# The mean square of the attention heads' outputs: two fp32r passes for each pair of blocks instead of fp32 products for a whole head

## The chip, the cores and the metric

The kernel runs on one core of one Trainium2 chip. The core has a matrix engine (TensorE, in the profile PE, with its weight loads as PEld), VectorE (DVE), ScalarE (ACT), GpSimd (POOL) and a queue of DMA issues (SyncE, SP). Each engine works through its own list of instructions in order, and waits on semaphores for the others. The metric is the time of one execution on the device in microseconds; lower is better.

## The reference, cut to what matters

One layer of a streaming encoder: an RMSNorm, a projection into eleven parts, a gated linear attention (GLA) branch, a differential attention branch, and their merge. The prompt has 1024 frames, the sample 32. The change touches one spot of the differential branch, the RMSNorm over the 128 channels of each head's output:

```python
def rmsnorm(x, g):
    xf = x.astype(F32)
    y = xf * lax.rsqrt(jnp.mean(xf * xf, axis=-1, keepdims=True) + EPS) * g.astype(F32)
    return y.astype(x.dtype)
...
    attn = p[:, :, 0] - lam * p[:, :, 1]
    return jnp.einsum('bhqk,bkhe->bqhe', attn, v.astype(F32))
...
    yd = (rmsnorm(o_diff.astype(x.dtype), diff_subln_g) * (1.0 - lambda_init)).reshape(B, T, DIFF_VAL) * jax.nn.silu(dg)
```

For each head (8) and each of the 1024 prompt frames, the mean of 128 squares is needed, then its inverse root, which scales the head's output before `w_proj_diff`.

## The kernel before, in words

Most products are done as three fp32r passes: each fp32 operand is split in a high part (rounded to fp32r, made on ACT) and a low part (the rest, a subtraction on DVE or POOL), and high x high, low x high and high x low are added up in PSUM. Channels lie on the 128 partitions, frames on the free axis.

The stages are: normalisation and the value projections (to about 200 us), GLA with the projections that it needs (to about 600), differential attention (to about 1190), then the two output projections and the last product. In GLA and differential attention, several threads share TensorE: the attention itself (`diff_main`), the sample's attention (`sample_thread`) and a filler of projections (`fill`, three passes of 352 columns for each of 8 blocks of channels, lines 465 to 467, 24 passes to a PSUM bank, two such banks). A small planner, `Order`, writes the order of TensorE: a step of a thread says what it costs, which events it needs and with which lag (the table `W`), and which PSUM banks it takes; the planner keeps a clock of these numbers and picks the first thread that is ready. TensorE is then run in that order as written. The other engines are ordered by the compiler's scheduler from priorities and the order in which the program was written.

One head of the differential attention, for 8 blocks of 128 frames: scores of both softmaxes (lines 883 and 884), the row maxima and the exponentials (887 on DVE, 889 on ACT), the difference of the two (892 to 894 on DVE), transposes (931) with the split of the transposed part (933 on ACT, 934 on DVE), and after each second block the value product of the pair (944 to 946) into a bank of the kind "o", of which there is one. ACT reads this bank twice: the squares go to `sqo` (947), the values to `osb` (948). At the end of a head, `diff_fin` averages the squares over the partitions: a product with a matrix whose entries are all 1/128 (`one_h`), twice 512 columns in fp32 (859), each into the one "o" bank; ACT reads one row of the result (860), and SP stores the 1024 averages (862). Then DVE multiplies the whole `osb` by the gate (865, 128x1024), and SP stores it. In `diff_main` the steps of `diff_fin` come after the next head's first scores. The values of the next head are split just then, the high part on ACT (912), the low part on POOL (913).

The sample thread, once for two heads, transposes its probabilities in two groups (1006), which ACT and DVE (1008, 1009) add up, before its value products (1018).

After the attention, the averages of all heads are read back, turned into scales on ACT, spread over the partitions (`rsb`) and multiplied into the outputs (1141) ahead of the second output projection (443 to 445). The first output projection (`pg_first`, 1099 to 1101) reads the GLA branch's gated tiles, split by 1069 (ACT) and 1070 (DVE).

## Time and profile before

| | us |
|---|---|
| median of 3 runs | 1483.13 |
| lowest, highest | 1480.83, 1486.48 |
| the profiled execution | 1483.59 |
| its span | 1481.9 |

The granted clock of TensorE over the profiled execution is 0.99 of full speed. In the lists, a row of the order of time gives the start, the duration, the engine, the line and the operation, what is written and read, and in brackets the idle time of the engine in front of it with what ended it. A row of a group gives the count, the busy time, the mean duration in ns, and the idle time in front. A row of stretches gives the length of the stretch, the busy time (and instructions) of PE, PEld, DVE, ACT and POOL, the granted clock, the DMA share and GB/s. The starts and ends of matmuls overlap by their pipeline, so the time that a row of passes takes is read from the distance of their starts.

### The profile page before, as it was taken

How to read it: one execution, taken by the hardware profiler on the slowest of the kernel's cores; microseconds unless marked ns; L12 is line 12 of the kernel's file. 1: busy time of each engine (PE TensorE's matmuls, PEld its weight loads, DVE VectorE, ACT ScalarE, POOL GpSimd, SP SyncE). 2: the span in 40 equal slices, each digit the busy share in tenths (PEclk: the TensorE clock that was granted, in tenths of full speed). 3: DMA queues.
4: the chain of work that ended last, by engine and by line, in shares of the span. 5: the costliest groups of instructions: out<-in, count | busy, mean ns of one | idle time of the engine just before them, and what ended most of it. 6: DMA issues, size and time to landing. Idle time of an engine off the chain costs nothing.

```text
span 1481.9 us, 22365 instructions
## 1 busy us (share of the span) xinstructions
PE 1422.6 (96%) x8848; PEld 1327.6 (90%) x8848; DVE 786.6 (53%) x1464; ACT 601.0 (41%) x1262; POOL 298.4 (20%) x186
## 2 busy tenths in 40 slices
PE   8999999989999999899999999999899899999997
PEld 6787789889989899899989998998899799999997
DVE  5702005755565343576767767678665535455415
ACT  5612114535344232455555555555455432221311
POOL 1200002222213224123222222222221111122001
PEclk9999999999999999999999999999999999999999
DMA  8621111122222233323232333223322278633205
GB/s 310 205 105 38 45 45 48 56 74 68 81 70 73 70 120 108 90 62 106 72 108 60 106 86 96 69 83 90 92 68 81 97 264 302 223 131 129 103 1 192
DMA packets 66742, 156.58 MB, mean 106 GB/s; under 512 B 10008, under 2 KB 28568, under 8 KB 65600
## 3 DMA queue, kind: packets, MB, share of 16 engines
q1 hardware_dynamic: 66624, 155.01, 32.3%
q8 instruction: 74, 1.21, 0.3%
q14 instruction: 44, 0.36, 0.1%
HBM read 104.39 MB, written 40.04 MB: 97 GB/s over the span
## 4 chain that ended last, share of the span: by engine, by line
PE 51%; DVE 6%; DMA 4%; ACT 2%; issue 1%; POOL 1%; SPq 0%; DVEq 0%; POOLq 0%; ACTq 0%
PE ps_w L465 9%; PE ps_w L466 9%; PE ps_w L467 9%; PE ps_w L444 2%; PE ps_w L443 2%; PE ps_w L445 2%; PE ps_s L884 2%; PE ps_t L931 2%; PE ps_s L883 2%; DMA ydr<-ydd 2%; PE ps_c L1193 2%; PE ps_c L1195 2%; PE ps_c L1194 2%; PE po L945 1%; PE po L946 1%
## 5 line engine op out<-in xcount | busy, mean ns | idle before, releaser
L465 PE MATMUL ps_w<-X,wh 128*128 128x352 f32 x1344 | 453.8, 338 | 8.5 <-DVE sg L478 3.2
L466 PE MATMUL ps_w<-X,wl 128*128 128x352 f32 x1344 | 438.2, 326 | 0.0
L467 PE MATMUL ps_w<-X,wh 128*128 128x352 f32 x1344 | 436.4, 325 | 0.0
L435 POOL TENSOR_TENSOR wl<-wr,wh 128x1024 fp32r<-128x1024 f32 x72 | 179.5, 2493 | 661.8 <-ACT wh L433 528.6
L465 PEld LDWEIGHTS ps_w<-X,wh 128*128 128x128 f32 x1344 | 255.8, 190 | 13.6 <-issue 4.9
L466 PEld LDWEIGHTS ps_w<-X,wl 128*128 128x128 f32 x1344 | 256.1, 191 | 1.2 <-issue 1.2
L467 PEld LDWEIGHTS ps_w<-X,wh 128*128 128x128 f32 x1344 | 255.1, 190 | 0.0
L889 ACT ACTIVATE p<-ps_s,nm 128x256 f32<-128x256 f32 (+7 forms) x128 | 94.6, 741 | 59.1 <-DVE ps_s L885 31.1
L286 PE MATMUL ps_v<-wh,X 128*128 128x512 f32 x248 | 97.6, 393 | 0.6 <-DVE X L225 0.6
L287 PE MATMUL ps_v<-wl,X 128*128 128x512 f32 x248 | 98.0, 395 | 0.0
L433 ACT ACTIVATE wh<-wr 128x1024 fp32r<-128x1024 f32 x72 | 75.9, 1054 | 54.6 <-PE ps_w L467 30.4
L285 PE MATMUL ps_v<-wh,X 128*128 128x512 f32 x248 | 97.9, 395 | 0.0
L887 DVE TENSOR_REDUCE nm<-ps_s 128x1 f32<-128x256 f32 (+7 forms) x128 | 94.8, 747 | 2.7
L272 DVE TENSOR_TENSOR vo<-ps_v,vo 32x512 f32<-32x512 f32 x4 | 2.7, 679 | 139.9 <-ACT vo L271 139.9
L885 DVE MEMSET ps_s<- 64x64 f32 x128 | 14.3, 112 | 115.8 <-PE ps_s L884 114.2
L650 POOL TENSOR_TENSOR vl<-vr,vh 128x512 fp32r<-128x512 f32 (+1 forms) x20 | 24.8, 1242 | 222.8 <-DVE t L516 160.3
L883 PE MATMUL ps_s<-k,q 128*128 128x512 f32 (+2 forms) x192 | 68.0, 362 | 1.2 <-DMA k<-k 1.2
L884 PE MATMUL ps_s<-kl,q 128*128 128x512 f32 (+2 forms) x192 | 63.8, 348 | 3.9 <-DMA kl<-kl 3.4
L268 ACT ACTIVATE vo<-ps_v 128x512 f32<-128x512 f32 x32 | 19.1, 596 | 114.2 <-PE ps_v L287 113.8
L933 ACT ACTIVATE ah<-ps_t 128x512 fp32r<-128x512 f32 (+2 forms) x96 | 46.9, 488 | 43.6 <-PE ps_t L931 43.0
L934 DVE TENSOR_TENSOR al<-ps_t,ah 128x512 fp32r<-128x512 f32 (+2 forms) x96 | 53.1, 554 | 18.6 <-ACT ah L933 17.3
L444 PE MATMUL ps_w<-Y,wl 128*128 128x352 f32 x192 | 62.2, 324 | 0.0
(319 smaller groups left out, 2960.9 us busy)
## 6 DMA issues: line engine op xcount, KB each, us to landing
wr<-w SPq DMA_DIRECT2D x72, 512.0 KB
thd<-gate SPq DMA_DIRECT2D x16, 528.0 KB
xn<-xn SPq DMA_DIRECT2D x16, 512.0 KB
wr<-wv SPq DMA_DIRECT2D x16, 512.0 KB
newk<-rr SPq DMA_DIRECT2D x8, 528.0 KB
ygr<-ygd SPq DMA_DIRECT2D x8, 528.0 KB
tha<-thd SPq DMA_DIRECT2D x8, 528.0 KB
ydr<-ydd SPq DMA_DIRECT2D x8, 528.0 KB
```

Of the source, the lines that this page charges most:

```text
L285: mm(ps, xk[:, 0, t0 : t0 + P], wh[:, k, :], start=(k == 0), stop=False)
L286: mm(ps, xk[:, 1, t0 : t0 + P], wh[:, k, :], start=False, stop=False)
L287: mm(ps, xk[:, 0, t0 : t0 + P], wl[:, k, :], start=False, stop=(k == KT - 1))
L435: nc.gpsimd.tensor_tensor(wl, wr, wh.bitcast(F32), op=ALU.subtract)
L444: mm(ps[:, :n], wl[:, k, :], src[k][:, 0, t0 : t0 + n], start=False, stop=False)
L465: mm(ps[:, :n], wh[:, k, :], src[k][:, 0, t0 : t0 + n], start=(k == 0), stop=False)
L466: mm(ps[:, :n], wl[:, k, :], src[k][:, 0, t0 : t0 + n], start=False, stop=False)
L467: mm(ps[:, :n], wh[:, k, :], src[k][:, 1, t0 : t0 + n], start=False, stop=(k == KT - 1))
L883: mm(ps[:, n0 : n0 + n], qs[m][:, qsl], ks[m][:, n0 : n0 + n], start=True, stop=False)
L884: mm(ps[:, n0 : n0 + n], qs[m][:, qsl], kls[m][:, n0 : n0 + n], start=False, stop=True)
L887: ve.tensor_reduce(nm, ps[:, 0:w], axis=AX.X, op=ALU.max, negate=True)
L889: act(p[:, 0:w], ps[:, 0:w], AF.Exp, bias=nm, accum_out=sm[:, m : m + 1])
```

## The change

The averages are made for each pair of blocks, 256 columns, rather than for 512 columns at the head's end. `diff_out` takes the place of the two reads of the value product: squares and values as before, then a tile `sqs` with the fp32r high part of the squares (ACT) and the low part (DVE). `diff_mean` multiplies both parts by `one_h`, now an fp32r matrix (1/128 is exact in it), in two passes into an "o" bank, and ACT reads one row of 256. The average of a pair stands in `diff_main` just ahead of the next pair's value product; that of the fourth pair is what is left in `diff_fin`. The planner is told 0.23 for such a step instead of 0.86, and a lag behind the value product that is longer by 1.0. `sqs` uses the one buffer that the sample's pairs use at other times. The matrix for the first, warming products is now a tile of its own (`one_f`), and two tiles of the lambda computation move from constant storage into buffers of the first stage.

```diff
-    one_h = cst.tile([P, P], F32, name="one_h")
-    ve.memset(one_h, 1.0 / P)
+    one_h = cst.tile([P, P], F32R, name="one_h")
...
+    one_f = v1.tile([P, P], F32, name="one_f")
+    ve.memset(one_f, 1.0 / P)
...
+        act(one_h, one_f, AF.Copy)
...
-        lv = cst.tile([P, 4, HD], F32, name="lv")
+        lv = v1.tile([P, 4, HD], F32, tag="xn", bufs=2, name="lv")
...
-    def diff_fin(h, osb, sqo):
-        for n0 in (0, 512):
-            yield 0.86, [(("pv", h, 3), W["pv"])], ["o"]
-            ps = obank("ps_m")
-            mm(ps, one_h, sqo[:, n0 : n0 + 512], start=True, stop=True)
-            act(sqo[0:1, n0 : n0 + 512], ps[0:1], AF.Copy)
-            S.free("o", W["m_o"])
+    def diff_out(g, po, osb, sqo):
+
+        sq = sqo[:, g * 256 : g * 256 + 256]
+        act(sq, po, AF.Square)
+        act(osb[:, g * 256 : g * 256 + 256], po, AF.Copy)
+        sqs = cst.tile([P, 2, 256], F32R, tag="pair", name="sqs")
+        act(sqs[:, 0], sq, AF.Copy)
+        ve.tensor_tensor(sqs[:, 1], sq, sqs[:, 0].bitcast(F32), op=ALU.subtract)
+        return sqs
+
+    def diff_mean(h, g, sqo, sqs):
+        yield 0.23, [(("pv", h, g), W["pv"] + 1.0)], ["o"]
+        ps = obank("ps_m")[:, 0:256]
+        mm(ps, one_h, sqs[:, 0], start=True, stop=False)
+        mm(ps, one_h, sqs[:, 1], start=False, stop=True)
+        act(sqo[0:1, g * 256 : g * 256 + 256], ps[0:1], AF.Copy)
+        S.free("o", W["m_o"])
+
+    def diff_fin(h, osb, sqo, sqs):
+        yield from diff_mean(h, 3, sqo, sqs)
         st(msd[h : h + 1, :], sqo[0:1, :])
...
+                if g:
+                    yield from diff_mean(h, g - 1, sqo, sqs)
                 yield 0.32 * (i + 0.5), [(("at", h, i), W["at"]), (("dv", h), W["dv"])], ["o"]
...
-                act(sqo[:, g * 256 : g * 256 + 256], po, AF.Square)
-                act(osb[:, g * 256 : g * 256 + 256], po, AF.Copy)
+                sqs = diff_out(g, po, osb, sqo)
                 S.free("o", W["pv_o"])
                 S.mark(("pv", h, g))
-            fin = diff_fin(h, osb, sqo)
+            fin = diff_fin(h, osb, sqo, sqs)
```

The planner's order moves with it. In the changed kernel the lines of this region have new numbers: the scores are 898 and 899, the memset and the row maximum 900 and 902, the gate product 880, the reciprocal and the two steps behind it 907 to 909, the transposes 946, the sample's transposes 1022 and their sum 1025, the projection passes 467 to 469, the average's two passes 870 and 871.

DVE at the end of the first head, before (885 and 887: the next head's first scores; 865: the gate product):

```order
L885 MEMSET ps_s 64x64
L887 TENSOR_REDUCE nm<-ps_s 128x1
L885 MEMSET ps_s 64x64
L887 TENSOR_REDUCE nm<-ps_s 128x1
L865 SCALAR_TENSOR_TENSOR osb<-osb,gs_half,sg 128x1024
L892 RECIPROCAL sm<-sm 128x2
L893 TENSOR_SCALAR p<-p,sm,neglam 128x128
```

and the same place in the changed kernel (864: the low part of the fourth pair's squares):

```order
L902 TENSOR_REDUCE nm<-ps_s 128x1
L900 MEMSET ps_s 64x64
L880 SCALAR_TENSOR_TENSOR osb<-osb,gs_half,sg 128x1024
L902 TENSOR_REDUCE nm<-ps_s 128x1
L864 TENSOR_TENSOR sqs<-sqo,sqs 128x256
L907 RECIPROCAL sm<-sm 128x2
L908 TENSOR_SCALAR p<-p,sm,neglam 128x128
```

The low part stands behind the gate product. At the ends of the second to seventh heads the row maximum stands ahead of the gate product and the reciprocal between it and the low part; the two stay in this order.

TensorE at the end of the first head, before (883, 884: the next head's first scores; 12 passes of projections are left out):

```order
L883 MATMUL ps_s<-k_7418,q_7049 128x128
L884 MATMUL ps_s<-kl_7420,q_7049 128x128
L465 MATMUL ps_w<-X_88,wh 128x352
...
L859 MATMUL ps_m<-sqo,one_h 128x512
L465 MATMUL ps_w<-X_88,wh 128x352
```

and in the changed kernel, where 18 passes of projections stand at the left-out place and 12 behind the average:

```order
L898 MATMUL ps_s<-k_7430,q_7051 128x128
L899 MATMUL ps_s<-kl_7432,q_7051 128x128
L467 MATMUL ps_w<-X_87,wh 128x352
...
L870 MATMUL ps_m<-sqs,one_h 128x256
L871 MATMUL ps_m<-sqs,one_h 128x256
L467 MATMUL ps_w<-X_87,wh 128x352
```

Before, a second product of 512 columns followed 12 passes later. The first new pass (870) waits for ACT, the second (871) for DVE; at the other averages of a head, which stand right behind a group of transposes, no wait on DVE is written.

TensorE at the end of the sixth head, where the sample thread has a part in it, before (1006: the sample's transposes):

```order
L884 MATMUL ps_s<-kl_11288,q_10924 128x128
L1006 MATMUL ps_st<-ident,p 128x128 x4
L465 MATMUL ps_w<-X_89,wh 128x352
...
L859 MATMUL ps_m<-sqo,one_h 128x512
L1006 MATMUL ps_st<-ident,p 32x128
L465 MATMUL ps_w<-X_88,wh 128x352
```

and in the changed kernel (6 passes are left out at the first place, 6 at the second):

```order
L870 MATMUL ps_m<-sqs,one_h 128x256
L871 MATMUL ps_m<-sqs,one_h 128x256
...
L1022 MATMUL ps_st<-ident,p 128x128 x4
L898 MATMUL ps_s<-k_11423,q_11035 128x256
L899 MATMUL ps_s<-kl_11425,q_11035 128x256
...
L898 MATMUL ps_s<-k_11424,q_11036 128x256
L899 MATMUL ps_s<-kl_11426,q_11036 128x256
L1022 MATMUL ps_st<-ident,p 32x128
```

The average now stands ahead of the sample's transposes, and scores and passes stand between their two groups.

## The prediction

> **What bounds the kernel now.** I read the page's totals first, then the busy time by stretches, then the instruction groups of the stretch that the change touches, then the waits of TensorE (PE) in it, and last the order of time around the places where the old averages stood.

> ```profile
> PE 1422.6 (96%) x8848; PEld 1327.6 (90%) x8848; DVE 786.6 (53%) x1464; ACT 601.0 (41%) x1262; POOL 298.4 (20%) x186
> 620.00:1195.00 575.00, 558.64 (x3582) 525.95 (x3581) 396.37 (x769) 301.38 (x685) 136.51 (x64) 0.99 0.29 87
> PE ps_st L1006 <- DVE smp L1009: 3.6, 2, 2.3
> ```

> The second row is the stretch of differential attention: 575 us, of which PE works 558.6, VectorE (DVE) 396, ScalarE (ACT) 301, GpSimd (POOL) 137. PE is the bound, and it runs an order written out by the planner. So a microsecond of PE work removed there is worth a microsecond, and a microsecond that PE's queue stands still costs one. The third row is one of the few waits of PE in this stretch; it matters below.

> **What the change removes and adds on PE.** Sixteen fp32 averages of 512 columns (line 859) go; 32 averages of 256 columns come, each as two fp32r passes. The first price is a piece of the chain of waits, and there are two such pieces in each head; the second is read from the value products of a head, which are fp32r passes of the same shape:

> ```profile
> 676.45 0.86 PE ps_m L859 x2
> L859 PE MATMUL ps_m<-sqo,one_h 128*128 128x512 f32 x32 | 17.3, 622 | 0.0
> 671.15 0.28 PE L944 MATMUL po<-ah,vh 128*128 128x256 f32 x1
> ...
> 673.47 0.28 PE L946 MATMUL po<-ah,vl 128*128 128x256 f32 x1
> ```

> An fp32 average shows as two records, so 32 records are 16 averages, of 0.86 us each: 13.8 us. From the first to the last of the two value rows lie 20 steps (21 passes) in 2.32 us: 0.116 us a pass. 64 passes cost 7.4 us. **Term 1: -6.4 us.**

> **What it adds on ACT and DVE.** For each pair of blocks ACT makes one more copy (the high part), DVE one subtraction (the low part), and ACT reads 256 instead of 512 averaged columns, twice as often.

> ```profile
> L947 ACT ACTIVATE sqo<-po 128x256 f32<-128x256 f32 x32 | 12.2, 380 | 41.3 <-PE po L946 38.1 <-issue 3.2
> L860 ACT ACTIVATE sqo<-ps_m 1x512 f32<-1x512 f32 x16 | 9.4, 586 | 18.4 <-PE ps_m L859 18.4
> L835 DVE TENSOR_TENSOR kl<-rr,k 64x256 fp32r<-64x256 f32 x28 | 11.6, 413 | 0.4
> L931 PE MATMUL ps_t<-ident,p 128*128 128x128 f32 x288 | 47.6, 274 | 7.0 <-DVE al L934 4.1 <-DVE smp L1032 1.7 <-DVE ps_s L885 0.9
> ```

> ACT: 32 copies at 0.38, plus 32 reads at about 0.38, minus 9.4, is 15 us more on an engine that is busy 301 of 575. DVE: 32 subtractions at 0.41 (the same operation on 256 columns) are 13 us more on 396. Both engines keep room on the average. In the middle of a head the average stands right behind a group of transposes, whole scores after its squares were made, and the order gives it no wait on DVE of its own there; so these 24 subtractions cost PE nothing unless they make the softmax late. Their cover is the fill of 18 projection passes, about 3 us, that the planner puts between a group of transposes and the value products. I put **term 2 at +1 us**; it lies between 0 and +8 (the upper end is priced with the rivals).

> **Where the wait goes: the head's end.** The fourth average of a head has no such distance. In the order it stands behind the next head's first scores and 18 projection passes, and its second pass waits for DVE. On DVE the subtraction stands behind the product of the whole head's output with its gate (line 865 before, 880 after). What these did at the end of the first head:

> ```profile
> 673.86 0.27 PE L883 MATMUL ps_s<-k,q 128*128 128x128 f32 x1
> 674.31 0.38 PE L465 MATMUL ps_w<-X,wh 128*128 128x352 f32 x1
> 676.29 1.02 PE L859 MATMUL ps_m<-sqo,one_h 128*128 128x512 f32 x2
> 673.95 1.06 ACT L912 ACTIVATE vh<-vr 128x1024 fp32r<-128x1024 f32 x1 [4.02 <-PE po L945]
> 675.18 0.38 ACT L948 ACTIVATE osb<-po 128x256 f32<-128x256 f32 x1
> 675.09 2.37 POOL L913 TENSOR_TENSOR vl<-vr,vh 128x1024 fp32r<-128x1024 f32 x1 [4.00 <-ACT vh L912]
> 674.92 0.29 DVE L887 TENSOR_REDUCE nm<-ps_s 128x1 f32<-128x128 f32 x1
> 675.59 2.96 DVE L865 SCALAR_TENSOR_TENSOR osb<-osb,gs_half,sg 128x1024 f32<-128x1024 f32 x1 [0.38 <-ACT osb L948]
> 678.47 0.15 DVE L892 RECIPROCAL sm<-sm 128x2 f32<-128x2 f32 x1
> ```

> Let T be 673.86, where the value products end and the scores begin. PE: 12 projection passes run from 674.31 to 676.29, 0.165 each, so 18 end at 677.28; the first pass of the average takes 0.12, and the second stands ready at 677.40, T + 3.5. DVE: the gate product starts at 675.59 and frees DVE at 678.47, T + 4.6. In the new order one short operation (0.15 or 0.29) comes next, then the subtraction of 0.41: it is ready at about 679.1, T + 5.2 to 5.3. PE waits some **1.75 us**, and nothing fills it, since its queue runs in order: behind the waiting pass stand projection passes, then the next scores. ACT, too, stands at its read of the average, and behind it one evacuation of a projection bank; of these banks there are two, and one bank takes 24 passes, so this is covered.

> ```profile
> L865 DVE SCALAR_TENSOR_TENSOR osb<-osb,gs_half,sg x8: 1285/2952/2974, 675.6 to 1182.5; 128x1024 f32<-128x1024 f32 x8
> 1182.48 1.28 DVE L865 SCALAR_TENSOR_TENSOR osb<-osb,gs_half,sg 128x1024 f32<-128x1024 f32 x1
> ```

> The gate product takes 1.28 us (minimum, at the last head, where POOL is idle beside it), 2.95 in the median, and 2.96 here, ending 1.1 us after POOL's subtraction (675.09 + 2.37 = 677.46). A wait on POOL is what makes the low part late. [...]

> Heads 1, 2, 4, 5 and 6 (counting from 1) I take to have these same distances, by the median of 2.95. At the ends of heads 3 and 7 PE is itself late by a transfer of keys:

> ```profile
> 818.66 0.33 PE L884 MATMUL ps_s<-kl,q 128*128 128x128 f32 x1 [0.57 <-DMA kl<-kl]
> 819.31 2.97 DVE L865 SCALAR_TENSOR_TENSOR osb<-osb,gs_half,sg 128x1024 f32<-128x1024 f32 x1
> 1113.10 0.37 PE L465 MATMUL ps_w<-X,wh 128*128 128x352 f32 x1
> 1116.27 0.15 DVE L892 RECIPROCAL sm<-sm 128x2 f32<-128x2 f32 x1
> ```

> There 18 passes behind the scores end at about 819.0 + 3.0 = 822.0, against DVE free at 819.31 + 2.9 = 822.2 and the low part at 822.9: a wait of about 0.9; and 1113.10 + 3.0 = 1116.1 against 1116.27 + 0.15 + 0.41 = 1116.8: about 0.6. The eighth head belongs to the tail. **Term 3: 5 x 1.75 + 0.9 + 0.6 = +10.3 us.** From below: if the gate product took its 1.28 us everywhere, DVE would be free 1.6 us sooner and the term would be nearly 0; from above, 2.1 us at each of seven heads, 14.7.

> **What the new order takes away.** At two head ends PE now waits for the sample thread's transposed probabilities (line 1009), and DVE is late with them for the same reason, the gate product in front of them:

> ```profile
> 748.01 0.28 PE L1006 MATMUL ps_st<-ident,p 128*32 128x128 f32 x1 [1.25 <-DVE smp L1009]
> 1039.30 0.37 PE L1006 MATMUL ps_st<-ident,p 128*32 128x128 f32 x1 [2.31 <-DVE smp L1009]
> 1039.00:1043.00 4.00, 3.70 (x14) 3.73 (x15) 0.97 (x4) 0.21 (x1) 0.00 (x0) 0.57 0.75 251
> 440.30 0.43 PE L465 MATMUL ps_w<-X,wh 128*128 128x352 f32 x1 [1.91 <-DVE sg L478]
> 440.00:444.00 4.00, 3.70 (x22) 3.43 (x22) 1.43 (x4) 1.29 (x2) 0.23 (x1) 1.00 0.00 1
> 499.06 0.40 PE L465 MATMUL ps_w<-X,wh 128*128 128x352 f32 x1 [2.06 <-PEq L579]
> 499.00:503.00 4.00, 3.94 (x16) 3.97 (x17) 2.80 (x5) 1.92 (x4) 0.00 (x0) 0.61 0.49 138
> ```

> In the new order the average, with its wait, comes first, the sample's transposes after it, and 6 projection passes and scores (1.4 us) between the first four and the fifth; the DVE step in between (ACT 0.4, DVE 0.4) fits under that. The waits of 1.25 and 2.31 go. The second one costs more than itself: over the 4 us behind it the granted clock is 0.57, so 4 x 0.43 = 1.7 us of full clock are missing. **Term 4: -5.3 us.** It lies between 0, if the sample's step is late again, and -5.3.

> **Clock.** By the same rows, a wait of 1.91 left the clock at 1.00, one of 2.06 halved it (0.61). My waits of 1.75 lie below, not by much; I take one of the seven to be long enough, **term 5: +1.7 us** (0 to 7 x 1.7 = 12). [...]

> **The tail.**

> ```profile
> 1183.47 0.43 PE L1099 MATMUL ps_w<-y,wh 128*128 128x352 f32 x1 [1.51 <-ACT y L1069]
> 1184.99 0.43 PE L1101 MATMUL ps_w<-y,wh 128*128 128x352 f32 x1 [0.93 <-DVE y L1070]
> 1268.83 1.25 DVE L1070 TENSOR_TENSOR Y<-ydr,Y 128x1056 fp32r<-128x1056 f32 x1
> 1285.88 0.16 PE ps_w L443
> ```

> At the last head the averages of pairs 3 and 4 stand apart, and two sample products and a transpose move behind the value products, into time in which PE waits anyway for the first gated tiles. The store queue (SP) takes the sample's last stores behind the loads of these tiles instead of between them, and the read of the averages behind those; the scaled outputs that hang on it (the last at 1270.1) are finished 15 us before the first product that reads them (1285.88), so some 4 us later cost nothing. **Term 6: -1 us** (-3 to +3). The constants' changes (one copy on ACT, one 128 KB load that leaves the ramp) I count at nothing: the copy runs while ACT waits for value tiles, and the load is one of some 500.

> **Sum.** -6.4 + 1 + 10.3 - 5.3 + 1.7 - 1 = +0.3. Against the profiled execution (1483.59 us; its span is 1481.9 and 1.7 lie around it) that is 1483.9. The median of the runs, 1483.13, is 0.5 us under the profiled one, so for the median 1483.4; I say **1484 us**.

> **Rivals.** *The low part comes in time* (faster). If POOL's subtraction runs at another moment, so that the gate product takes 1.28 us, term 3 and term 5 vanish: -6.4 + 1 - 5.3 - 1 = -11.7, **1472 us**. [...] Against: six of the eight gate products show the long form, and nothing in the change moves POOL there. Chance 0.17.

> *Each head's end halves the clock* (slower). Place: the second pass of the fourth average. It decides once the wait reaches about 2.0 us (1.91 did not, 2.06 did), 0.25 more than I work out. Price: 7 x 1.7 instead of one, plus 0.3 on five waits: +11.7, **1495 us**. For it: the threshold is near and the phase of the waits is unknown. Against: 1.25 and 1.91 left the clock alone, and heads 3 and 7 have short waits. Chance 0.17.

> *The subtractions in mid head meet POOL* (slower or same). POOL is busy 137 of 575 us in pieces of 2.4 to 2.5; one subtraction in four meets one and stands 1.2 us, DVE loses 24 x 0.3 = 7 us, and if PE has no slack, +6: **1490 us**. Against it: before 288 transposes PE waits 7.0 us in all, so the softmax has slack now. [...] Chance 0.10.

> That the change does nothing on PE I exclude: the order shows 64 passes of 256 columns where 16 products of 512 stood.

> **Chances.** Forecast 0.56, early low part 0.17, clock 0.17, mid head 0.10. A measurement of this kernel tells about 0.5% (7.4 us) from no change, that is, outside 1475.7 to 1490.5. Faster: 0.17. Slower: all but 0.02 of the clock rival and half of mid head, 0.20. Same: the rest, 0.63. The forecast's own range is 1478 to 1490; for 8 in 10 I take in most of both neighbours: **1473 to 1493**.

> **What would show it.** In the new profile: the groups of the two average lines with 64 passes and some 7 us of spacing; a wait of PE at the second average's line on the low part, seven times, in sum about 10 us (right), or near 0 (first rival) or above 14 with a clock near 0.6 behind it (second); no wait at the sample's transposes; the gate product still near 2.96. Wrong would be PE idle elsewhere in the stretch: at the transposes (mid head) or behind 1185 us (tail).

## The result: 1.6% slower, and where the 23 us went

| | before | after |
|---|---|---|
| median, us | 1483.99 | 1507.49 |
| lowest, highest | 1480.83, 1489.53 | 1505.69, 1509.81 |
| span of the profiled execution | 1481.9 | 1504.7 |

The ratio is 1.0155, with an interval of 1.0133 to 1.0177. Forecast were 1484 us and a range of 1473 to 1493; the time lies outside it.

First the stretch that the prediction took for the bound, and the one behind it, in the changed kernel (length, busy time of PE, PEld, DVE, ACT and POOL, granted clock, DMA share, GB/s):

```profile
620.00:1195.00 575.00, 546.50 (x3541) 522.14 (x3541) 400.44 (x792) 302.56 (x719) 132.80 (x63) 0.99 0.27 79
1195.00:1300.00 105.00, 99.11 (x588) 95.83 (x587) 42.97 (x54) 34.26 (x42) 19.21 (x9) 0.93 0.75 264
```

PE is busy 546.5 of 575 us, 12 less than before, with 41 fewer passes done in that stretch, so the engine that was to gain time stands still more often. Its waits from 600 to 1290 us, from the list of waits (total, times, longest):

```profile
PE ps_t L946 <- DVE smp L1048: 14.0, 3, 4.7
PE ps_m L871 <- DVE sqs L864: 6.3, 5, 1.5
PE ps_s L899 <- DMA kl<-kl: 5.4, 7, 2.2
PE ps_t L946 <- DVE al L949: 3.1, 2, 2.4
PE ps_st L1022 <- DVE al L949: 2.3, 1, 2.3
PE ps_t L946 <- DVE p L909: 2.1, 2, 1.1
PE ps_w L1115 <- ACT y L1085: 2.0, 1, 2.0
```

The second row is the wait that the prediction names (term 3). The first is not in it: three waits of some 4.6 us at a group of transposes, on VectorE's last step of the sample thread (line 1048, the two heads' gated products; 1032 before). Before, the same wait stood once, with 1.7 us. The waits at the sample's transposes on its sum (3.6 us before) are gone, as forecast.

Here is the first of the three. VectorE, in order of time:

```profile
780.83 0.25 DVE L1048 SCALAR_TENSOR_TENSOR smp<-ps_so,gs_half,smp 128x32 f32<-128x32 f32 x1
781.41 0.11 DVE L900 MEMSET ps_s<- 64x64 f32 x1 [0.33 <-PE ps_s L899]
...
784.69 0.69 DVE L818 SCALAR_TENSOR_TENSOR q<-rr,q 64x512 fp32r<-64x512 f32 x1
785.41 0.69 DVE L820 SCALAR_TENSOR_TENSOR q<-rr,q 64x512 fp32r<-64x512 f32 x1
786.13 0.17 DVE L907 RECIPROCAL sm<-sm 128x2 f32<-128x2 f32 x1
786.21 0.23 DVE L1048 SCALAR_TENSOR_TENSOR smp<-ps_so,gs_half,smp 128x32 f32<-128x32 f32 x1
786.36 0.60 DVE L908 TENSOR_SCALAR p<-p,sm,neglam 128x640 f32<-128x640 f32 x1
```

and TensorE, with the clock over the 4 us behind the wait:

```profile
781.74 0.27 PE L899 MATMUL ps_s<-kl,q 128*128 128x128 f32 x1
786.59 1.03 PE L946 MATMUL ps_t<-ident,p 128*128 128x128 f32 x4 [4.57 <-DVE smp L1048]
...
786.50:790.50 4.00, 3.91 (x17) 3.94 (x18) 2.04 (x3) 0.86 (x2) 0.00 (x0) 0.57 0.03 4
```

The two products of 32 columns read one PSUM bank. The first runs at 780.83. The second stands ten places further down VectorE's list, behind two memsets, two row maxima, four steps of the next head's queries and a reciprocal: it runs at 786.21, and VectorE works nearly all the time between. Until then the bank of kind "t", of which there is one, is not free, and the next transposes need it. Before the change the two stood one, two and seven places apart at these three places; here is the first, where they follow each other (x2):

```profile
770.90 0.40 DVE L1032 SCALAR_TENSOR_TENSOR smp<-ps_so,gs_half,smp 128x32 f32<-128x32 f32 x2
```

The one wait of 1.7 us before stands at the third place, the one with seven. In the changed kernel TensorE stands 4.57 us and then runs at half clock (0.57 over the 4 us). It is the same in heads 3, 5 and 7 and nowhere else, since the sample's step comes once in two heads.

From the first scores to the end, the two profiles differ by 1504.7 - 605.7 = 899.0 against 1481.9 - 600.3 = 881.6, that is 17.4 us. It nearly adds up: the waits on the second product +12.3, on the low part +6.3, the sample's old waits -3.6, the average's passes -6.4 (below), the clock +8.5 (in the trace's clock records TensorE spends 30.7 us at half clock in this part against 13.7: three times 3.4 us behind the new waits, once behind a wait of 2.39 on `al` at 745 us, once behind the first scores' wait for keys as before, the rest, 13.7, behind 1195 us): 17.1. The other waits change by 0.2 in sum. The remaining 5.4 us lie ahead of the first scores; more on them below.

### The profile page after: what moved, and what is told of

The parts are those of the page before. It is cut to its first block, busy times and chain, and to the rows that moved or that the text cites. A ratio compares the mean times of both kernels' runs of the same rounds, so it can differ in the third digit from the quotient of the medians.

```text
span 1504.7 us, 22497 instructions
## 1 busy us (share of the span) xinstructions
PE 1426.3 (95%) x8880; PEld 1336.1 (89%) x8880; DVE 792.6 (53%) x1496; ACT 609.5 (41%) x1311; POOL 296.1 (20%) x186
## 4 chain that ended last, share of the span: by engine, by line
PE 50%; DVE 11%; ACT 2%; DMA 1%; issue 1%; POOL 1%; SPq 0%; DVEq 0%; POOLq 0%; ACTq 0%
PE ps_w L467 9%; PE ps_w L468 9%; PE ps_w L469 9%; PE ps_w L446 2%; PE ps_w L445 2%; PE ps_w L447 2%; PE ps_t L946 2%; PE ps_s L899 2%; PE ps_s L898 2%; PE ps_c L1209 2%; PE ps_c L1211 2%; PE ps_c L1210 2%; DVE nm L902 1%; DVE osb L880 1%; PE po L962 1%
## 5 line engine op out<-in xcount | busy, mean ns | idle before, releaser
L437 POOL TENSOR_TENSOR wl<-wr,wh 128x1024 fp32r<-128x1024 f32 x72 | 176.3, 2449 | 643.4 <-ACT wh L435 578.2
L946 PE MATMUL ps_t<-ident,p 128*128 128x128 f32 x288 | 49.1, 281 | 19.3 <-DVE smp L1048 14.0
L948 ACT ACTIVATE ah<-ps_t 128x512 fp32r<-128x512 f32 (+2 forms) x96 | 46.6, 486 | 49.9 <-PE ps_t L946 49.4
```

The source lines that it names most:

```text
L437: nc.gpsimd.tensor_tensor(wl, wr, wh.bitcast(F32), op=ALU.subtract)
L946: nc.tensor.transpose(ps[:, (j - j0) * P : (j - j0 + 1) * P], p[:, j * P : j * P + P], ident)
```

## Experiments

All ratios are against the kernel before, run beside each experiment on the same chip.

| run | median, us | ratio | interval |
|---|---|---|---|
| before, again (e5), one execution | 1482.46 | | |
| after, again (e6) | 1508.36 | 1.0164 | 1.0147 to 1.0182 |
| e1 constants of the change alone | 1485.45 | 1.0021 | 1.0006 to 1.0035 |
| e2 after, constants as before | 1511.60 | 1.0185 | 1.0168 to 1.0201 |
| e3 after, sample's products first | 1496.34 | 1.0090 | 1.0075 to 1.0105 |
| e4 after, low part early | 1491.10 | 1.0051 | 1.0033 to 1.0068 |
| e7 new places, old fp32 averages | 1485.97 | 1.0010 | 0.9998 to 1.0021 |
| e8 after, no low part | 1478.04 | 0.9950 | 0.9931 to 0.9968 |
| e9 as e8, squared once | 1480.85 | 0.9969 | 0.9954 to 0.9985 |
| e10 e4 and e3 with more cover | 1528.09 | 1.0294 | 1.0263 to 1.0326 |
| e11 still more cover | 1551.76 | 1.0458 | 1.0427 to 1.0489 |
| e12 before with more cover and the sample's products first | 1511.58 | 1.0185 | 1.0159 to 1.0211 |
| e13 e4, POOL in pieces | 1496.04 | 1.0074 | 1.0052 to 1.0096 |
| e14 before, POOL in pieces | 1491.53 | 1.0043 | 1.0027 to 1.0060 |
| e15 after, POOL in pieces | 1506.34 | 1.0136 | 1.0115 to 1.0157 |
| e16 e4, pieces in the differential stage | 1481.92 | 0.9980 | 0.9966 to 0.9993 |
| e17 e8, pieces in the differential stage | 1468.27 | 0.9895 | 0.9878 to 0.9911 |
| e18 before, pieces in the differential stage | 1479.03 | 0.9959 | 0.9942 to 0.9975 |

### The stretch ahead of the first scores (e1, e2, e5, e6)

Between 58 and 100 us the value products stood 233 ns apart in the changed kernel and 229 before, and the first scores came 5.5 us later, in code that the change hardly touches. The moved constants shift the addresses of all tiles behind them. So e1 makes that move alone in the kernel before:

```diff
-    ve.memset(one_h, 1.0 / P)
...
+    one_f = v1.tile([P, P], F32, name="one_f")
+    ve.memset(one_f, 1.0 / P)
...
+        act(one_h, one_f, AF.Copy)
...
-        lv = cst.tile([P, 4, HD], F32, name="lv")
+        lv = v1.tile([P, 4, HD], F32, tag="xn", bufs=2, name="lv")
...
-        lp = cst.tile([P, 2, HD], F32, name="lp")
+        lp = v1.tile([P, 2, HD], F32, tag="xr", bufs=2, name="lp")
```

> The kernel before, with only the constants moved as in the change: the table of 1/128 is made in the value stage's pool and copied by ScalarE, the two lambda tables lie in the slots of that pool, so the tiles behind lie 1,536 bytes lower (activations) and 1,024 bytes lower (value weights). The averages are the old fp32 ones. Theory (addresses): the value products read their two operands at another distance; their spacing goes from 229 to 233 ns as in the changed kernel, the value stage ends 3.2 us later, the first scores 3 to 5.5 us later, and nothing happens behind them: 1487 to 1490 us. Rival (the shift ahead of the differential stage belongs to the new order): 1484 us, first scores' wait at 602.8.

and e2 undoes it in the changed kernel (the fp32r table takes the slot of `lp`, when that has been read):

```diff
-    one_h = cst.tile([P, P], F32R, name="one_h")
+    one_f = cst.tile([P, P], F32, name="one_f")
+    ve.memset(one_f, 1.0 / P)
...
+        lp = cst.tile([P, 2, HD], F32, tag="lp", name="lp")
...
+        one_h = cst.tile([P, P], F32R, tag="lp", name="one_h")
+        act(one_h, one_f, AF.Copy)
```

> The changed kernel, with the constants laid out so that every other tile has its address of before (the fp32r table takes the slot of the second lambda table). The order of every engine's work is otherwise that of the changed kernel. Theory (addresses): the spacing of the value products is 229 ns again, the first scores' wait stands at 602.8 to 604 instead of 608.2, and the rest is as in the changed kernel with its three waits of 4.6 us behind the sample's products: 1502 to 1504 us. Rival (the shift comes from the order): 1507 us.

The theory of addresses fell. With the addresses of the change, e1 shows 229 ns; with those of before, e2 shows 229 ns too, but its first scores start at 606.2 and it is no faster than the changed kernel. Nor do the constants set the spacing in the later runs: e12, with those of before, shows 233 ns, and e17, with those of the change, 229. e1 costs 0.2% (0.06 to 0.35%), which bounds what the constants are worth: about 3 us, 5 at most. Then the two kernels themselves were profiled once more:

> The kernel before, profiled a second time. If the stretch ahead of the first scores of differential attention is the same in every execution, its first scores start at 600.3 us again (within 0.5), and the 602 to 606 us of the other kernels are theirs. If it differs from one execution to the next, they start up to 3 us or more later here too.

> The changed kernel, on the same chip as the other runs of this group. By the first theory its first scores start at 605.7 us again and the three waits of 4.6 us, the five to seven on the low part and the four to five halvings stand where they stood: 1505 to 1510 us. By the rival (the shift ahead differs by execution) the start lies anywhere from 601 to 608, and the rest is the same.

```profile
602.35 0.30 PE L883 MATMUL ps_s<-k,q 128*128 128x128 f32 x1 [1.17 <-DMA k<-k]
```

```profile
604.26 0.30 PE L898 MATMUL ps_s<-k,q 128*128 128x128 f32 x1 [1.18 <-DMA k<-k]
```

The kernel before (first row) starts its first scores at 602.35 here and at 600.26 in the profile before; the changed kernel (second row) at 604.26 and 605.73. Over all profiles of kernels whose first stages are the same (all but e13 to e15) the start lies between 600.3 and 608.8, and e17 below, which has all of the changed constants, starts at 600.64. So a part of the 5.5 us is the scatter between executions, and a part, by e1 and by the medians, may be real. Which, and by what, stays open. What repeats is the rest: from the first scores on, the second pair differs by 1503.3 - 604.3 = 899.0 against 1480.7 - 602.4 = 878.4, 20.6 us; the waits of 14.0 us and those on the low part (6.7) are there again, and TensorE spends 27.3 us at half clock in this part against 6.8.

### The sample's products and the low part (e3, e4)

e3 gives the two products the main thread's priority, so that they stand two apart:

```diff
-                ve.scalar_tensor_tensor(y, pt[:, (h - h0) * NS : (h - h0 + 1) * NS], gs_half, sgs[h],
-                                        op0=ALU.mult, op1=ALU.mult)
+                with first():
+                    ve.scalar_tensor_tensor(y, pt[:, (h - h0) * NS : (h - h0 + 1) * NS], gs_half, sgs[h],
+                                            op0=ALU.mult, op1=ALU.mult)
```

> The changed kernel, with the sample thread's two gated products (line 1048) given the main thread's priority, so that they stand two apart on VectorE and not ten; TensorE's order is the same instruction for instruction. Theory (the second product is late and holds the transposes' bank): the three waits of 4.6 us go (14.0) and with them three halvings of the clock (3 x 1.7): 1507.5 - 19 = 1488 us; the waits on the low part stay near 6. Rival (VectorE is loaded too heavily, so that a wait removed there comes back at the next transposes): a gain under 6 us, 1502 or more.

e4 makes the low part early: ScalarE takes the high part straight from PSUM, so that VectorE finds the low part ready before the gate product.

```diff
+        sqs = cst.tile([P, 2, 256], F32R, tag="pair", name="sqs")
+        act(sqs[:, 0], po, AF.Square)
         act(sq, po, AF.Square)
         act(osb[:, g * 256 : g * 256 + 256], po, AF.Copy)
-        sqs = cst.tile([P, 2, 256], F32R, tag="pair", name="sqs")
-        act(sqs[:, 0], sq, AF.Copy)
```

> The changed kernel, with the high part taken by ScalarE from PSUM as a square of its own, ahead of the fp32 square and the copy of the output. The same number of instructions; the low part now stands ahead of the gate product on VectorE at each head's end, and the sample's two products stand next to each other as well. TensorE's order is unchanged. Theory (both places): the waits on the low part (6.3 us) and the three of 4.6 us with their halved clock (19 us) go: about 1482 us, 6 below the run before it in this series. Rival (the gate product, now later, makes another wait of the same size): equal to that run, 1488.

In both, TensorE's order is that of the changed kernel. Waits of TensorE in e3:

```profile
PE ps_t L946 <- DVE p L909: 7.6, 5, 2.0
PE ps_m L871 <- DVE sqs L864: 6.5, 6, 1.5
```

and in e4:

```profile
PE ps_t L946 <- DVE p L909: 7.8, 5, 2.1
...
PE ps_m L871 <- DVE sqs L864: 0.6, 2, 0.3
```

The wait on the second product is gone in both, and nearly all of the wait on the low part in e4 as well. e3 gains (1.0164 - 1.0090) x 1484 = 11 us, not 19; e4 another 5.2 us, near the 6 expected, though both stay 8 to 9 us above the times of their theories. Neither theory for e3 had the number: most of the gain is real, but 5.5 us come back as waits on the softmax's probabilities (2.1 before e3, 7.6 in it). The three new ones stand at the three places where the longer wait had been. And e4, at 1491, is still 0.5% slower than the kernel before, with 0.6 us left of the waits that the prediction names.

### Why the probabilities are late (e7, e8, e9)

One of the five places in e4, VectorE:

```profile
783.16 0.61 DVE L908 TENSOR_SCALAR p<-p,sm,neglam 128x640 f32<-128x640 f32 x1
783.81 2.87 DVE L820 SCALAR_TENSOR_TENSOR q<-rr,q 64x512 fp32r<-64x512 f32 x1
786.71 0.88 DVE L909 SCALAR_TENSOR_TENSOR p<-p,sm 128x640 f32<-128x640 f32 x1
```

POOL and TensorE at that time:

```profile
783.71 2.42 POOL L437 TENSOR_TENSOR wl<-wr,wh 128x1024 fp32r<-128x1024 f32 x1 [13.20 <-ACT wh L435]
...
787.65 0.33 PE L946 MATMUL ps_t<-ident,p 128*128 128x128 f32 x1 [1.70 <-DVE p L909]
```

POOL's subtraction for a projection weight (line 437) starts at 783.71, and the step of the queries that VectorE starts 0.10 us later takes 2.87 us instead of the 0.69 of its like. The probabilities behind it are ready 9.0 us after the scores' end (778.57), and the transposes stand there after 7.4. At the other four places it is the same POOL instruction, beside this step or beside the probabilities' own; in the first two heads, which have no such wait, it starts 1.4 and 0.4 us behind the scores' end instead of 5.0 to 5.5. Three kernels ask what of the change brings this about. In e7 the fp32 averages stay and only the places are new:

```diff
-        mm(ps, one_h, sqs[:, 0], start=True, stop=False)
-        mm(ps, one_h, sqs[:, 1], start=False, stop=True)
+        mm(ps, one_h, sqs, start=True, stop=True)
```

(This is the difference to the changed kernel; `sqs` is here the slice of fp32 squares itself, and nothing is split.)

> The kernel before, with its fp32 averages put at the new places (one per pair of blocks, 256 columns, 0.43 us each) and nothing else of the change: no high and low part, no fp32r passes, constants as before. TensorE's order is that of the changed kernel but for one fp32 pass where two fp32r passes stand. On VectorE the sample thread's two products stand seven apart at three places. Theory (the new places shift the phase and that makes the waits): waits of 2 to 4 us at those three transposes, with halved clock, and one or two near 2 us at the others: 1491 to 1500 us. Rival (the work added on VectorE and ScalarE makes them): no wait over 1.7 us, 1480 to 1486.

e7 takes the time of the kernel before (1.0010, with 1 inside the interval): the places alone cost 0.2% at most, and no wait on the probabilities is in its list, though the profile is of the slowest of its twelve executions (1494.39 us). The sample's two products stand seven places apart in it at all three places, for three waits of 2.8 us in sum. (TensorE's order was not wholly that of the changed kernel: the planner's other cost, 0.43, puts a few pieces around the sample's step and in the tail elsewhere. So e7 tells that such places can be had for nearly nothing, not that each piece is innocent.) In e8 the subtraction and its pass are missing:

```diff
-        ve.tensor_tensor(sqs[:, 1], sq, sqs[:, 0].bitcast(F32), op=ALU.subtract)
...
-        mm(ps, one_h, sqs[:, 0], start=True, stop=False)
-        mm(ps, one_h, sqs[:, 1], start=False, stop=True)
+        mm(ps, one_h, sqs[:, 0], start=True, stop=True)
```

> The changed kernel without the low part: ScalarE's high part and one fp32r pass stay, VectorE's 32 subtractions and the 32 second passes are left out, so the averages are those of the rounded squares. The sample's two products stand next to each other again. TensorE's order is otherwise unchanged. Theory (the subtractions make the waits): the waits at the low part (6.3) go, those of 4.6 too (14 + 5 of clock), those on the softmax's probabilities (5 left in the run with the sample product first) as well, and 3.7 us of passes: 1507 - 34 = 1473 to 1478 us. Rival (the order makes them, by laying weights' low parts on the softmax): the waits on the probabilities stay at 5 to 8 us: 1480 to 1485.

and in e9 ScalarE's additional copy as well:

```diff
-        act(sq, po, AF.Square)
-        act(sqs[:, 0], sq, AF.Copy)
+        act(sqs[:, 0], po, AF.Square)
```

> As the kernel without the low part, and without the fp32 square as well: ScalarE squares straight into the fp32r tile, so it makes two operations per pair of blocks as before the change, and VectorE none. Left out: the low part, as there. TensorE's order is that of the changed kernel less 32 passes, so six projection passes still lack between the value products and the next scores behind the sample's step. Theory (lost cover: 7.4 us from scores to transposes where 8.5 stood before): the waits on the softmax's probabilities stay, 4 to 7 us: 1476 to 1480. Rival (ScalarE's 32 more operations make them): they go, 1470 to 1473.

The list of waits of e8, then of e9:

```profile
PE ps_t L944 <- DVE p L907: 6.5, 5, 1.6
```

```profile
PE ps_t L941 <- DVE p L904: 6.6, 5, 1.6
```

The five waits stay, with neither the subtractions nor the copies. So neither piece of the added work makes the probabilities late by itself; what is common to e4, e8 and e9 is the moment at which POOL's subtraction falls. In e7 it falls 0.2 us behind the scores' end at these places. Which piece moves it there was not isolated, since e7 differs from e9 in the averages' length on TensorE and in some places of the order. Nor was the theory of e9 tested apart, that fewer passes stand between scores and transposes there. e8 has the time of its theory but not the reason, since that had the five waits go. It is 30 us faster than the changed kernel, which is about what the waits tied to the low part amount to: 14.0 + 5.1 (three halvings) + 6.7 + 3.7 (32 passes of 0.116) = 29.5, with smaller items of both signs beside them.

### More cover, tried through the planner (e10, e11, e12)

If the transposes come 1 us too early, the planner can be told a longer lag. e10 is e4 and e3 together with that number, e11 goes further (3.5), and e12 is the kernel before with the number of e10 and the priority of e3.

```diff
-    ... "sm_s": 2.25, "p": 2.4, "p_w": 0.00204,
+    ... "sm_s": 2.25, "p": 3.0, "p_w": 0.00204,
```

> The changed kernel whole, with three edits: high part from PSUM ahead of the fp32 square (low part early), the sample's products at the main thread's priority, and the planner's lag for the softmax's probabilities 3.0 us instead of 2.4, which puts six projection passes back between scores and transposes at those places. Theory (lost cover): of the 7.8 us of waits on the probabilities 1 us goes at each of five places, and halvings with them: 1491 - 5 to 8 = 1483 to 1486 us. Rival (VectorE behind the transposes stays the bound, the wait moves on): 1489 to 1492.

> The same with a lag of 3.5 us: twelve projection passes at some of these places. Theory (lost cover): the rest of the waits on the probabilities goes, 1479 to 1484. Rival (the passes taken there lack elsewhere): the same as with 3.0 or slower.

> The kernel before with the planner's lag at 3.0 us alone: what that edit is worth without the change. Theory (before had its cover already): no gain, 1482 to 1487. Rival (a larger lag helps any order): 1475 to 1480.

All three missed: 1528, 1552 and 1512 us. In e10 the largest rows of the list of waits are

```profile
PE ps_t L946 <- DVE al L949: 11.6, 10, 2.1
PE ps_st L1022 <- DVE smp L1025: 8.5, 4, 6.1
```

These are waits at other transposes. The new lag also changes the places of hundreds of projection passes, and the kernel before pays 1.9% for the same two edits. So this says nothing on the cause; it shows how steeply the time depends on the written order. How much of the 28 us in e12 is the lag's alone was not tried: the priority of e3 is in it too.

### POOL in four pieces (e13 to e18)

The next edit moves nothing on TensorE or VectorE. POOL's subtractions are written as four of 256 columns:

```diff
-        nc.gpsimd.tensor_tensor(wl, wr, wh.bitcast(F32), op=ALU.subtract)
+        for k in range(0, KT, 2):
+            k2 = slice(k, k + 2)
+            nc.gpsimd.tensor_tensor(wl[:, k2], wr[:, k2], wh[:, k2].bitcast(F32), op=ALU.subtract)
```

> The kernel with the low part early, with GpSimd's subtractions (low parts of weights and values, 1,024 columns, 2.4 us) each in four pieces of 256 columns. The orders of TensorE and VectorE are the same instruction for instruction. Theory (an instruction of VectorE beside one of GpSimd is held until the latter ends): none is held longer than some 0.7 us, the probabilities are ready 7 us behind the scores' end instead of 8.2 to 9.4, the waits on them fall from 7.8 us to under 2, two halvings go with them: 1491 - 6 to 10 = 1481 to 1485 us. Rival (both share the memory, and the bytes count): VectorE loses as much in all, and it stays at 1489 to 1492.

> The kernel before, with GpSimd's subtractions in four pieces and nothing else. Theory (held until the end): the gate products take 1.3 to 2 us instead of 2.95, the waits at the sample's transposes (1.25 and 2.31) and some at the others shrink: 3 to 6 us less, 1478 to 1481. Rival (bytes count, or the waits have other causes): 1483 to 1486.

> The changed kernel, with GpSimd's subtractions in four pieces and nothing else. Theory (held until the end): the gate product at each head's end takes 1.3 to 2 us instead of 2.95, so the waits on the low part behind it fall from 6.3 us to under 2.5; the three waits behind the sample's products stay (14.0), since these come from VectorE's order: 1508 - 4 to 7 = 1501 to 1504 us. Rival: waits on the low part as before, 1506 to 1510.

The waits fell as forecast and the times did not. In e15, the changed kernel with pieces, the wait on the low part behind the gate product is all but gone, and the gate product is short:

```profile
PE ps_t L950 <- DVE smp L1052: 13.7, 3, 4.6
...
PE ps_m L873 <- DVE sqs L866: 0.6, 2, 0.3
```

```profile
L882 DVE SCALAR_TENSOR_TENSOR osb<-osb,gs_half,sg 128x1024 f32<-128x1024 f32 x8 | 11.2, 1396 | 4.8 <-ACT osb L863 4.8
```

This is 1.40 us in the mean. The same group in the changed kernel takes 2.59:

```profile
L880 DVE SCALAR_TENSOR_TENSOR osb<-osb,gs_half,sg 128x1024 f32<-128x1024 f32 x8 | 20.8, 2594 | 6.2 <-ACT osb L861 6.2
```

The wait on the sample's second product stays at 13.7, as it must if VectorE's order makes it. In e13 the five waits on the probabilities (7.8 us) fall to three of 1.2 us in sum. From the first scores on, the pieces gain in all three: 880.0 us in e13 against 881.9 in e4, 876.5 in e14 against 881.6 and 878.4 before, 894.6 in e15 against 899.0. But each weight now takes POOL four times 0.8 us instead of 2.45, and the first scores of e13 to e15 start at 610 to 616 us: the earlier stages, which have such subtractions too, seem to pay. Hence the pieces in the differential stage alone:

```diff
+    pieces = [slice(0, KT)]
...
+        for k2 in pieces:
+            nc.gpsimd.tensor_tensor(wl[:, k2], wr[:, k2], wh[:, k2].bitcast(F32), op=ALU.subtract)
...
+    pieces[:] = [slice(k, k + 2) for k in range(0, KT, 2)]
...
+    pieces[:] = [slice(0, KT)]
```

(The third cut stands ahead of differential attention, the last behind it.)

> The kernel with the low part early, with GpSimd's subtractions in four pieces for the weights and values of differential attention alone; the earlier stage and the last one as in the changed kernel. The orders of TensorE and VectorE are the same. Theory (the earlier stage paid for the pieces): first scores at 604 to 606 us again, and from there 880 us as in the run with pieces everywhere: 1486 to 1489 us. Rival (the pieces cost in this stage as much as they give): 1491 to 1496.

> The same pieces in the kernel without the low part (one fp32r pass of the rounded squares; the low part and its pass are left out). Theory: the five waits on the probabilities (6.5 us, with one or two halvings) go: 1478 - 5 to 8 = 1470 to 1473 us. Rival: 1477 to 1480.

> The same pieces in the kernel before. Theory: its gate products are shorter, the waits at the sample's transposes (3.6 us) go: 1484 - 3 to 5 = 1479 to 1481 us. Rival: 1483 to 1486.

All three times are below the ranges of their theories or at the lower end, and their first scores start at 605.2, 600.6 and 605.1 us again. e16, from the list of waits and from the order of time on POOL and VectorE at the place shown for e4:

```profile
PE ps_t L951 <- DVE p L913: 1.2, 3, 0.4
```

```profile
782.15 4.06 POOL L440 TENSOR_TENSOR wl<-wr,wh 128x256 fp32r<-128x256 f32 x4 [13.20 <-ACT wh L437]
...
782.25 1.19 DVE L824 SCALAR_TENSOR_TENSOR q<-rr,q 64x512 fp32r<-64x512 f32 x1
783.47 1.25 DVE L913 SCALAR_TENSOR_TENSOR p<-p,sm 128x640 f32<-128x640 f32 x1
784.65 0.95 DVE L868 TENSOR_TENSOR sqs<-sqo,sqs 128x256 fp32r<-128x256 f32 x1
```

VectorE's step beside POOL takes 1.19 us where it took 2.87, and POOL's four pieces take 4.06 here (four times 0.84 in the mean of e16 from 620 to 1195 us) where one took 2.42: VectorE's step is shorter and POOL's work longer. e16 has the whole computation of the change and ends at 0.9980 of the kernel before (0.9966 to 0.9993), 1.8% under the change as it was. Against the kernel before with the same pieces (e18, 0.9959) it is 2.9 us behind in the median, with intervals that overlap. So with all three kinds of waits mended the change comes out about even; its 6 us on TensorE are used up elsewhere, and where was not taken apart. Without the low part (e17) it is 0.9895, the fastest here, at the price of averages of rounded squares.

## Why the prediction was wrong

**What bounds the kernel** was right: TensorE's order, where a standing microsecond is a microsecond lost. All that follows is such standing.

**Term 1 (-6.4) was right.** Where projections follow a group of transposes, the third pass starts 0.44 us behind the last transpose, and 0.67 with a new average between: 0.23 us for an average. An old one stretches a row of projections by 0.86. 32 x 0.23 - 16 x 0.86 = -6.4.

**Term 2 (+1, up to +8) is the step that failed.** "These 24 subtractions cost PE nothing unless they make the softmax late" looked for the price at the softmax and found cover there. The price came up at an operation that the change does not name. With the 32 subtractions where the change puts them, the scheduler lists the second of the sample's products ten places behind the first, and that instruction holds a PSUM bank of which there is one. (In e8, without the subtractions, and in e4, with the low part elsewhere, the two are neighbours; the new places alone, in e7, put them seven apart.) Cost: 14.0 us of waits where 1.7 stood, and some 5 of clock, of which e3 gives back 11 net. This could be read before the run: the new list of VectorE shows the two products ten apart. The prediction read that list at the heads' ends only. It also priced the rival "mid head" by the new subtractions meeting POOL. They do: seven of the 32 take 0.9 to 1.6 us beside a POOL instruction instead of 0.4, 6 us in all, near the rival's 7, but TensorE has no wait on them in mid head. What it waits for are old steps of the softmax and the queries that run beside POOL: two waits of 1 us here, five of 0.9 to 2.1 in e4, 1.2 us left of them in e16.

**Term 3 (+10.3) was right in its chain of waits and too large.** The low part is late behind the gate product, and that is long beside POOL (2.59 us in the mean, 1.40 with POOL in pieces): e4 and e15 remove most of it from either end (6.3 to 0.6 us). Five waits of 1.02 to 1.53 us were measured, at the ends of heads 2 to 6, where seven were forecast, five of them of 1.75. At the first head's end a wait for keys (0.72 us) just ahead covers it; at the seventh's, with waits for keys of 0.54 and 0.60 ahead, there is none either.

**Term 4 (-5.3) was right by 3.6.** The two waits at the sample's transposes went. The 1.7 us of clock behind one of them was no property of the kernel, as the last section shows. A wait of 2.29 us at the sample's transposes in the last head came instead (on `al`, above).

**Term 5 (+1.7) went by a rule that does not hold.** None of the waits on the low part halved the clock. From the first scores' own on, the halvings came behind the three long waits, one of 2.39 us, and in the tail. The last section shows the wait of 1.91 that the prediction took as harmless halving the clock in another execution.

**Term 6 (-1) had the wrong sign.** Behind 1195 us the changed kernel's clock is 0.93: the wait of 2.29 at the transposes and those of 2.00 and 0.99 for the first gated tiles (before 1.51 and 0.93) come close together, and 13.7 us at half clock follow, against 3.4. That is 5 us more; the second profiles show 10.2 against none. The constants, counted at nothing, are worth 3 us by e1, 5 at most.

**The rivals.** That each head's end halves the clock did not happen. The chance of "slower", 0.20, was too low for a reason that has no rival in the list: a change of VectorE's order away from the changed lines.

## What to carry to other kernels

When a scheduler orders an engine, read its new list at every place where that engine frees a single buffer that the bound engine needs, not only where the change's own instructions stand; two readers of one PSUM bank belong next to each other (or in one instruction, which was not tried here). Here a GpSimd instruction of 2.4 us let a VectorE step beside it take 2.9 instead of 0.7, so cutting it in pieces helped in the stage where TensorE waits for VectorE (e16), and the same cut in the earlier stages seems to have cost more than it gave (e13 to e15). A saving of 0.4% on the bound engine is smaller than what a new operation on another engine can undo by its place alone, so what the new operation stands in front of is worth more study than what it replaces.

## What the runs showed of the hardware

**The same wait halved the clock in one execution and not in another.** In the second profile of the kernel before, the same wait of 2.31 us as in the first, and in the second profile of the changed kernel the same wait of 1.91 us that the prediction shows at 440.30:

```profile
1041.00 0.27 PE L1006 MATMUL ps_st<-ident,p 128*32 128x128 f32 x1 [2.31 <-DVE smp L1009]
...
1040.70:1044.70 4.00, 3.70 (x22) 3.25 (x23) 1.16 (x7) 0.81 (x3) 0.00 (x0) 1.00 0.79 249
...
443.13 0.43 PE L467 MATMUL ps_w<-X,wh 128*128 128x352 f32 x1 [1.91 <-DVE sg L480]
...
443.10:447.10 4.00, 3.97 (x16) 3.97 (x17) 0.93 (x2) 1.02 (x2) 0.00 (x0) 0.62 0.00 0
```

**A VectorE step with one input tile took longer beside POOL as well.** In e8 the step of line 906 (a TENSOR_SCALAR of 128x640, which reads one tile and two scalars) takes 2.68 us beside POOL's 2.42, and 0.60 in the changed kernel at a free moment:

```profile
781.84 2.42 POOL L437 TENSOR_TENSOR wl<-wr,wh 128x1024 fp32r<-128x1024 f32 x1 [13.01 <-PE po L961]
...
781.92 2.68 DVE L906 TENSOR_SCALAR p<-p,sm,neglam 128x640 f32<-128x640 f32 x1
```

The prediction had looked at the gate product and the subtractions only. With POOL's work in four pieces, in e16, the three VectorE steps beside it take 1.19, 1.25 and 0.95 us, where their like take 0.69 (e16, at 779.56), 0.88 and 0.42 (e4, at 786.71 and 787.51) with POOL idle. These are durations; how one engine holds up the other was not shown.
